# The head of the first load by two queues, and the second load as one transfer

## The chip, the cores and the metric

The kernel runs on one core of a Trainium2 chip. The time is device microseconds of that core, as the median of several executions: 83.15 us over 7 runs, from 82.97 to 83.2. One more execution was profiled. It took 83.2 us itself, and the profile covers 81.4 us of it, from the first instruction to the last; all times inside the kernel are counted from the start of that span.

## The reference

The input is a matrix of 1024 rows and 4096 columns in float32. Each row has its mean taken off and every element is squared:

```python
mean = np.mean(x, axis=axis, keepdims=True)
return ((x - mean) ** 2).astype(np.float32)
```

So 16.78 MB are read from HBM, 16.78 MB are written, and a row's result can't be started until the whole row is there.

## The kernel before

The rows are taken as two tiles of 512 rows. In a tile each of the 128 partitions holds four whole rows one after the other, 4 x 4096 floats or 64 KiB, which lie side by side in HBM too. Both tiles fit into SBUF at once, so each has its own buffer (`bufs=ntiles`), nothing is used twice, and results overwrite the inputs in place.

All loads are issued ahead of any work, from two engines' DMA queues. The queue of SP (SyncE) is called q1 in the profile and that of ACT (ScalarE) q10. In the order of each queue:

- SP, line 52: the head of tile 0, the first 512 floats (2 KiB) of each partition.
- SP, line 53: the rest of tile 0, 62 KiB of each partition.
- SP, line 57: all of tile 1 but its last 512 floats, 62 KiB of each partition.
- ACT, line 56: the tail of tile 1, the last 2 KiB of each partition. It is the first thing in ACT's program.

Then the loops run over the two tiles and over the four rows of a partition. DVE (VectorE) adds the two halves of a row and sums them with the factor -1/4096, so that one instruction gives the negative mean (line 66). ACT squares the row with that number as its bias (line 77). Of each tile's fourth row ACT squares only the first 3584 columns; DVE does the last 512 (lines 86 and 87). When a tile's four rows are done, SP stores it in one DMA of 64 KiB a partition (line 88).

The first instruction on a tile waits for every DMA of the tile that it needs. For tile 0 that is the head and the rest together, since row 0 is 16 KiB wide and the head is only 2 KiB of it. The tail of tile 1 is needed only by that tile's fourth row. The stores wait in SP's queue until the last squares of their tile are written; behind the second store is nothing but the end of the program. The order on each engine is that of the program text: DVE's is held by `keep_in_program_order`, and the others follow their dependences.

Of the kernel before, what the change touches and what calls it, by code (L numbers as in the profile page):

```python
# [2 lines left out]

os.environ.setdefault("NEURON_RT_ULTRASERVER_MODE", "4")

# [4 lines left out]

F32 = mybir.dt.float32
ACT = mybir.ActivationFunctionType
ADD = mybir.AluOpType.add


@with_exitstack
def kernel(
    ctx: ExitStack,
    tc: tile.TileContext,
    x: bass.AP,  # L20
    axis: bass.AP,
    out: bass.AP,
):

    nc = tc.nc

    B, D = x.shape
    P = nc.NUM_PARTITIONS
    Q = 4
    HEAD = 512
    HALF = D // 2
    LAST = D - D // 8
    assert B % (P * Q) == 0
    ntiles = B // (P * Q)
    inv_d = 1.0 / float(D)

    x_t = x.rearrange("(p n q) d -> n p (q d)", p=P, q=Q)
    out_t = out.rearrange("(p n q) d -> n p (q d)", p=P, q=Q)

    io = ctx.enter_context(tc.tile_pool(name="io", bufs=ntiles))
    scratch = ctx.enter_context(tc.tile_pool(name="scratch", bufs=1))
    stats = ctx.enter_context(tc.tile_pool(name="stats", bufs=ntiles * Q))

    tiles = []
    for i in range(ntiles):
        x_tile = io.tile([P, Q * D], F32)  # L50
        if i == 0:
            nc.sync.dma_start(out=x_tile[:, :HEAD], in_=x_t[i][:, :HEAD])  # L52
            nc.sync.dma_start(out=x_tile[:, HEAD:], in_=x_t[i][:, HEAD:])  # L53
        else:
            end = Q * D - HEAD
            nc.scalar.dma_start(out=x_tile[:, end:], in_=x_t[i][:, end:])
            nc.sync.dma_start(out=x_tile[:, :end], in_=x_t[i][:, :end])
        tiles.append(x_tile)

    inorder = tc.keep_in_program_order  # L60
    for i in range(ntiles):
        for q in range(Q):
            row = tiles[i][:, q * D:(q + 1) * D]
            pairs = scratch.tile([P, HALF], F32)
            neg_mean = stats.tile([P, 1], F32)
            inorder(nc.vector.tensor_tensor_reduce(  # L66
                out=pairs,
                in0=row[:, :HALF],
                in1=row[:, HALF:],
                scale=-inv_d,  # L70
                scalar=0.0,
                op0=ADD,
                op1=ADD,
                accum_out=neg_mean,
            ))
            cut = D if q < Q - 1 else LAST
            nc.scalar.activation(  # L77
                out=row[:, :cut],
                in_=row[:, :cut],
                func=ACT.Square,  # L80
                bias=neg_mean,
                scale=1.0,
            )
            if cut < D:
                rest = row[:, cut:]
                nc.vector.tensor_scalar_add(out=rest, in0=rest, scalar1=neg_mean)  # L86
                nc.vector.tensor_mul(out=rest, in0=rest, in1=rest)  # L87
        nc.sync.dma_start(out=out_t[i], in_=tiles[i])


# [1 line left out]
_INS = ['x', 'axis']  # L92
_OUTS = [((1024, 4096), 'float32')]

_NUMBERS = {'axis': -1}


# [26 lines left out]
```

## Time and profile before

| What | Value | Where it is read |
|---|---|---|
| median of 7 runs | 83.15 us (82.97 to 83.2) | the times |
| profiled execution | 83.2 us | the times |
| its span | 81.4 us | head of the page |
| DVE busy | 20.8 us (25%) | part 1 of the page |
| ACT busy | 29.4 us (36%) | part 1 |
| DMA moved | 33.55 MB, 412 GB/s over the span | part 3 |
| first DMA issued | 0.73 us | timeline |
| store of tile 0 issued | 39.71 us | timeline |
| store of tile 1 issued | 58.3 us | answer for line 88 |

The row of digits after "DMA" cuts the span into 40 slices of about 2 us. A packet is counted in the slice in which it starts, and most packets here last longer than 2 us, so a low digit between two nines isn't idle time: the packets of all 16 DMA engines begin close together, and some slices hold fewer beginnings. The mean over ten or more slices can be trusted, a single slice can't. The same holds for the GB/s row and for short windows.

### The profile page before, as it was taken

The page shows a single profiled execution, that of the slowest core. Times are in us where ns is not written, and L with a number is a line of the kernel's source. Part 1 is how long each engine was busy: PE and PEld are TensorE (multiplying, and loading weights), DVE is VectorE, ACT ScalarE, POOL GpSimd, SP SyncE. Part 2 cuts the span into 40 slices and gives each one's busy share as a digit, 9 for nine tenths or more (in the row PEclk, how much of TensorE's full clock was granted, in tenths as well). Part 3 has the DMA queues.
Part 4 walks back from the last instruction along what each step waited for, and adds up shares of the span by engine and source line. Part 5 has one row for each costly group of instructions (what it writes and reads, how often), then busy time and mean ns, then how long its engine had stood idle before and what let it go on. Part 6 is the DMA issues. An engine that isn't in the chain of part 4 may idle for free.

```text
span 81.4 us, 87 instructions
## 1 busy us (share of the span) xinstructions
DVE 20.8 (25%) x20; ACT 29.4 (36%) x9; POOL 0.2 (0%) x4
## 2 busy tenths in 40 slices
DVE  0000000000059999500049999700000000000000
ACT  0000000000054999999402999999600000000000
POOL 0000000000000000000000000000000000000000
DMA  1994999999839999996599997599999299999480
GB/s 24 701 437 187 405 499 499 499 499 468 374 156 499 499 499 499 499 468 281 250 515 515 515 515 322 225 483 515 515 515 483 97 451 515 515 515 483 193 354 0
DMA packets 864, 33.55 MB, mean 412 GB/s; under 512 B 96, under 2 KB 96, under 8 KB 352
## 3 DMA queue, kind: packets, MB, share of 16 engines
q1 hardware_dynamic: 720, 33.29, 94.8%
q10 hardware_dynamic: 144, 0.26, 1.0%
HBM read 16.78 MB, written 16.78 MB: 412 GB/s over the span
## 4 chain that ended last, share of the span: by engine, by line
DMA 49%; ACT 13%; ACTq 4%; DVE 3%; SPq 1%; issue 0%
DMA x_tile<-in_x_dram 49%; ACT x_tile L77 13%; ACTq L119 4%; DVE pairs L66 3%; SPq L53 1%; SPq L52 0%; DVE neg_mean L66 0%
## 5 line engine op out<-in xcount | busy, mean ns | idle before, releaser
L77 ACT ACTIVATE x_tile<-x_tile,neg_mean 128x4096 f32<-128x4096 f32 (+1 forms) x8 | 28.2, 3590 | 5.6 <-DVE neg_mean L66 5.6
L66 DVE CUSTOM_DVE_ANT_0 pairs<-x_tile 128x2048 f32<-128x2048 f32 x8 | 18.3, 2292 | 31.6 <-DMA x_tile<-in_x_dram 31.3
L77 ACT ACT_TABLE_LOAD x1 | 1.3, 1283 | 23.2 <-DMA x_tile<-in_x_dram 23.2
L87 DVE TENSOR_TENSOR x_tile<-x_tile 128x512 f32<-128x512 f32 x2 | 1.4, 693 | 0.1
L86 DVE TENSOR_SCALAR x_tile<-x_tile,neg_mean 128x512 f32<-128x512 f32 x2 | 1.0, 487 | 0.1
L66 DVE DVE_READ_ACCUMULATOR2_ANT neg_mean<- 128x1 f32 x8 | 0.7, 82 | 0.0
L105 POOL MEMSET const-bfloat16-1.0<- 128x1 bf16 x1 | 0.1, 101 | 0.0
L105 POOL MEMSET const-uint8-127<- 128x1 uint8 x1 | 0.1, 101 | 0.0
L105 POOL MEMSET const-float32-0.0<- 128x1 f32 x1 | 0.1, 98 | 0.2 <-issue 0.2
L105 POOL MEMSET const-float32-1.0<- 128x1 f32 x1 | 0.1, 98 | 0.0
## 6 DMA issues: line engine op xcount, KB each, us to landing
x_tile<-in_x_dram SPq DMA_DIRECT2D x2, 7936.0 KB, 31.1
x_tile<-in_x_dram SPq DMA_DIRECT2D x1, 256.0 KB, 3.6
x_tile<-in_x_dram ACTq DMA_DIRECT2D x1, 256.0 KB, 3.8
out_dram<-x_tile SPq DMA_DIRECT2D x2, 21.9
```

What stands on the lines that cost most here:

```text
L53: nc.sync.dma_start(out=x_tile[:, HEAD:], in_=x_t[i][:, HEAD:])
L66: inorder(nc.vector.tensor_tensor_reduce(out=pairs, in0=row[:, :HALF], in1=row[:, HALF:], scale=-inv_d, scalar=0.0, op0=ADD, op1=ADD, accu ...
L77: nc.scalar.activation(out=row[:, :cut], in_=row[:, :cut], func=ACT.Square, bias=neg_mean, scale=1.0,)
L86: nc.vector.tensor_scalar_add(out=rest, in0=rest, scalar1=neg_mean)
L87: nc.vector.tensor_mul(out=rest, in0=rest, in1=rest)
L105: nc = _bacc.Bacc("TRN2", target_bir_lowering=False, num_devices=1)
L119: with _tile.TileContext(nc) as tc:
```

## The change

The head of tile 0 is still the first 2 KiB of each partition. It now comes as two DMAs: SP issues it for partitions 0 to 63, ACT for partitions 64 to 127. ACT no longer issues a tail for tile 1. Tile 1 is one DMA on SP, 64 KiB a partition. The rest of tile 0 stays as it was, second in SP's queue. There are four loads before and after, three from SP and one from ACT. One empty line of the source falls away as well, and the loop of the head is a line longer, so that later line numbers are lower by one in the changed kernel.

```diff
         if i == 0:
-            nc.sync.dma_start(out=x_tile[:, :HEAD], in_=x_t[i][:, :HEAD])
+            for queue, p in ((nc.sync, 0), (nc.scalar, P // 2)):
+                part = slice(p, p + P // 2)
+                queue.dma_start(out=x_tile[part, :HEAD], in_=x_t[i][part, :HEAD])
             nc.sync.dma_start(out=x_tile[:, HEAD:], in_=x_t[i][:, HEAD:])
         else:
-            end = Q * D - HEAD
-            nc.scalar.dma_start(out=x_tile[:, end:], in_=x_t[i][:, end:])
-            nc.sync.dma_start(out=x_tile[:, :end], in_=x_t[i][:, :end])
+            nc.sync.dma_start(out=x_tile, in_=x_t[i])
         tiles.append(x_tile)
```

The first instruction on tile 0 now waits for three DMAs (two halves of the head and the rest) where it waited for two. The first on tile 1 waits for one, which brings the fourth row's tail too. The order of the instructions on DVE, ACT and POOL is unchanged; only the sizes of the DMAs that SP and ACT issue differ.

## The prediction

> **What bounds the kernel now.** I read the page first, then the chain that ended last, the timeline of the issues, the waits of SP's queue, and last the single DMA packets of the trace. The page, part 1 to 3:
>
> ```profile
> DVE 20.8 (25%) x20; ACT 29.4 (36%) x9; POOL 0.2 (0%) x4
> ...
> DMA  1994999999839999996599997599999299999480
> ...
> q1 hardware_dynamic: 720, 33.29, 94.8%
> q10 hardware_dynamic: 144, 0.26, 1.0%
> ```
>
> No engine works half of the time, and the packets of the two queues fill 95.8% of all 16 DMA engines' span. What little they leave lies at the two ends. The chain that ended last (start, length, what):
>
> ```profile
> 1.15 0.43 SPq L53
> 1.58 0.05 issue
> 1.63 40.25 DMA x_tile<-in_x_dram
> ...
> 41.90 2.29 DVE pairs L66
> ```
>
> It runs through the second load (landing at 41.88) and then over DVE and ACT. That tail is misleading, because the second store has slack, as SP's waits (total, times, longest) and the timeline (start, length) show:
>
> ```profile
> SPq L119 <- DMA out_dram<-x_tile: 21.8, 2, 19.3
> SPq L88 <- ACT x_tile L77: 11.7, 2, 5.8
> ```
>
> ```profile
> 0.73 0.38 SPq L52 DMA_DIRECT2D x_tile<-in_x_dram  x1
> 0.73 0.40 ACTq L56 DMA_DIRECT2D x_tile<-in_x_dram  x1
> 1.15 0.43 SPq L53 DMA_DIRECT2D x_tile<-in_x_dram  x1
> 1.63 0.42 SPq L57 DMA_DIRECT2D x_tile<-in_x_dram  x1
> ```
>
> At the end SP waits for a store 21.8 us, 19.3 of them in one piece: transfers end the kernel, not arithmetic. The last store is issued at 58.31, while the packets of the first store drain from the 16 engines only between 60.15 and 60.94.
>
> The packet records settle it. Each DMA engine runs 16 packets of 2 KiB (eight of the head, eight of the tail), then eight of 62 KiB, eight more of 62 KiB, and twice eight of 64 KiB. Once an engine has begun its first long packet, the next begins as the one before ends: 2.342 us for 62 KiB, 2.418 us for 64 KiB, with at most 0.4 us of idle time on the few engines that wait for the first store. The last completion record of an engine lies between 79.47 and 80.28; the span ends 1.14 us after the latest. So the end is the start of the slowest engine plus a fixed amount of work. The 16 engines begin their first long packet between 3.34 and 4.07, and the one at 4.07 (the next is at 3.87) is also the one that ends at 80.28. How they come to that point, by windows (the last two columns: share of the DMA engines, GB/s):
>
> ```profile
> 1.10:1.70 0.60, 0.00 (x0) 0.00 (x0) 0.00 (x0) 1.00 0.00 0
> 1.70:2.30 0.60, 0.00 (x0) 0.00 (x0) 0.00 (x0) 1.00 0.71 147
> 2.30:3.30 1.00, 0.00 (x0) 0.00 (x0) 0.00 (x0) 1.00 0.99 338
> ```
>
> First packet 1.74 (1.01 us after the issue at 0.73), for ACT's queue 1.97; a slow 0.6 us, with single packets of 0.3 to 0.56 us; from 2.3 full. Within the full stretch a 2 KiB packet follows the last after 0.080 us. Only what happens before about 4 us, and the bytes, can move the time.
>
> **What the Trainium skill says.** "DMA: Bandwidth & Descriptors", section "Issuing engines are not separate DMA queues": transfers from SP and ACT run on the same 16 engines and interleave. The trace agrees: on the engine that starts last, packets of q1 and q10 alternate every 0.080 us. The same page, "Why a DMA increments its semaphore by 16 and not by 1": a transfer uses the largest number of engines up to 16 that divides its slowest dimension, so 64 partitions should still use 16, with four packets each; no run shows that yet. Its "Rules for kernel authors" say of two transfers to disjoint partition halves: "Don't bother — they serialize". And "SBUF — State Buffer", section "Door 1", gives 196 GB/s for partitions 0 to 63 alone (8 ports) against 328 GB/s for 128, both at 1 MiB. The kernel before has no half-width transfer, so its trace can't confirm these two.
>
> **The change, part by part**, on one DMA engine.
>
> 1. The tail leaves ACT's queue. Eight packets of 2 KiB go: 8 x 0.080 = 0.64 us less.
> 2. Tile 1 comes as packets of 64 KiB: 8 x (2.418 - 2.342) = 0.61 us more. The 2.418 is measured on stores; 2.342 x 64/62 = 2.418 says the same for loads.
> 3. The head stays at eight packets (four from each queue, 8 x 0.080 = 0.64). A second completion record comes with each half, as the tail had one: nothing.
> 4. SP's and ACT's issues: each queue keeps its number of DMAs, at 0.38 to 0.43 us each, so the rest of tile 0 is issued at about 1.15 and tile 1 at 1.63, as now. Nothing is moved past another instruction. If a 64-partition issue is shorter, SP's later ones gain some 0.1 us at most. ACT's table load behind its DMA waits until 23.2 for tile 0, which hides anything there.
> 5. Waits: the first DVE instruction needs three DMAs instead of two. The head halves land near 4 us, the rest at about 22.6, so the added wait is long met. Behind it is DVE's whole work, but the rest decides. Row 3 of tile 1 gets its tail with the load at 41.9 instead of early; DVE reaches that row only at 48.90, so this is covered by 7 us, and row 0 waits for that same load now as before.
> 6. What comes earlier: tile 0 lands 0.64 us sooner (23.2 to about 22.6), as no tail packets stand before it, and its store is issued at about 39.07 instead of 39.71. The first packet of this store came 1.13 us after its issue, on other engines up to some 1.55. Now the load of tile 1 is drained at 40.83 to 41.50 and a few engines wait up to 0.4 us; afterwards the store is ready in time everywhere. The slowest engine did not wait (its gap was 0.02), so this is worth nothing to the end. Tile 1's chain, landing to store in 58.31 - 41.88 = 16.43 us, keeps its length and its slack.
> 7. The unknown: is the engine fed when only 0.64 us of small packets stand before the rest of tile 0? Before, it had 1.28. The rest was issued at 1.15; with the delay of the head (1.01) and of the slowest engine of the store (1.55) its descriptors are there at 2.16 to 2.70. The earliest small packets start at 1.74, the slowest engines' near 2.07, and slow first packets add about 0.4 us on average (first long packet at 3.57 on average, less 1.85 for the start and 1.29 for the packets). So small packets last until 2.4 at the least, about 2.9 in the mean. I take the bubble as nothing. Ends: if descriptors came only at the moment at which each long packet now starts, the whole 0.61 us would be lost. On the other side, [...]the slowest engine could fall back in line with the next one: 4.07 - 3.87 = 0.2 us gained.
>
> Sum: -0.64 + 0.61 = -0.03 us. From the profiled 83.2 that is 83.17; this execution lies 0.05 above the median, so against the 83.15 shown it is 83.12.
>
> **The rivals.**
>
> *Slower: the start isn't filled.* The place is 1.7 to 4.1 us on the slowest engine, the price up to +0.61 us (83.76), and it counts from the point at which that engine's first long packet starts later than 4.07 - 0.61 = 3.46. The mechanism is the half-width transfer: if two halves share what eight ports take, 262 KB at 196 GB/s last 1.34 us (estimate from "SBUF — State Buffer") instead of 0.64. Since long packets for all partitions join at 2.2 to 2.7, only about 0.6 us of that is at half speed: +0.3 us, 83.45. For it: the page's rule, and ACT's queue starting 0.23 us late, so that SP's half is alone at first. Against it: the two queues together cover all partitions, and the first 0.6 us run at 147 GB/s anyway, below the 196 of one half.
>
> *Faster: a more even start.* Half as many descriptors for each queue and half as many slow small packets bring the slowest engine to its first long packet 0.2 us nearer to the others: -0.03 - 0.2 gives 82.92. For it: the end follows one straggler, 0.25 us behind the next engine (80.28 against 80.04). Against it: long single packets come with the first accesses of each engine on each queue, and both queues stay.
>
> *The tail's removal exposes a wait.* Tile 1 lands later as its load is longer by 0.61 us, so the second store starts later. The landing, 41.88, is the sum over an engine of the same bytes, so it doesn't move; the slack of 60.15 - (58.31 + 1.55) = 0.3 us on the first engine covers it. Time 83.12, not to be told from the main case.
>
> **How the numbers follow.** Main case (with the last rival) 53 in 100, its own range 82.99 to 83.31, which is within 0.2% or 0.17 us of the median, about what a measurement of this kernel can tell from no change. Slower 30, 83.32 to 83.76 and mostly near 83.45. Faster 17, 82.85 to 82.98. The range that leaves out about 2 in 10 cuts the outer part of both: 82.92 to 83.55.
>
> **What would show it.** Right: q1 with 656 packets and q10 with 80 (16 engines for each half); tile 0 landing near 22.6 and its store issued near 39.1; tile 1 landing at 41.8 to 42.0; long packets back to back from about 3.4 on the slowest engine; the last store issued near 58.3. Wrong: fewer completions for a half (then it uses fewer engines); gaps between small and first long packets, or small packets of 0.16 us (the ports); a first long packet after 3.6 on the slowest engine; a store of tile 1 that finds its engines idle near 60. A changed time with the start at 3.4 and the landing at 41.9 would refute the whole reading, for it would come from the stores.

## The result, and the profile after

The changed kernel takes 83.51 us (median of 13 runs, 83.28 to 84.47) against 83.14 for the kernel before (33 runs, 82.92 to 83.37). The ratio is 1.0065, with a 95% interval from 1.0047 to 1.0084: slower by about half a microsecond in the mean and by 0.37 in the median. The ratios here and below compare means and leave out single executions more than 1.5% above the fastest of their kernel, which the medians keep. The stated range held the time, but only in the part that a rival with another mechanism had put there; the likeliest case, no measurable change, was wrong.

The profiled execution took 83.44 us with a span of 81.6, so it shows 0.24 us of the loss. The page of the changed kernel, parts 1 to 3:

```profile
DVE 20.8 (25%) x20; ACT 29.4 (36%) x9; POOL 0.2 (0%) x4
...
DMA  0997499999938999974999992999995599999190
...
q1 hardware_dynamic: 656, 33.42, 95.2%
q10 hardware_dynamic: 80, 0.13, 0.5%
```

The arithmetic is the same to the digit. The packets are the 656 and 80 that 16 engines for each half give. The DMA row now begins with a 0 in its first slice where the kernel before had a 1. The timeline of the issues (start, length, queue and line) says a part of why:

```profile
0.72 0.54 SPq L53 DMA_DIRECT2D x_tile<-in_x_dram  x1
0.72 0.55 ACTq L53 DMA_DIRECT2D x_tile<-in_x_dram  x1
1.31 0.56 SPq L54 DMA_DIRECT2D x_tile<-in_x_dram  x1
1.94 0.42 SPq L56 DMA_DIRECT2D x_tile<-in_x_dram  x1
```

The kernel before issued its head in 0.38 us, the tail in 0.40 and the rest of tile 0 in 0.43. A half of the head, with half the bytes, keeps its queue for 0.54 or 0.55 us, and the DMA behind it on SP, which is the same as before, takes 0.56. Only tile 1's is back at 0.42. By windows (last two columns: share of the DMA engines, GB/s) nothing moves before 2 us:

```profile
1.70:2.00 0.30, 0.00 (x0) 0.00 (x0) 0.00 (x0) 1.00 0.00 0
2.00:2.30 0.30, 0.00 (x0) 0.00 (x0) 0.00 (x0) 1.00 0.88 177
```

SP's first packet starts at 2.04 instead of 1.74, ACT's at 2.40 instead of 1.97. On SP 0.16 us of the 0.30 are the longer issue; the rest lies between the end of the issue and the first packet, and what it is the trace doesn't show. The chain and the waits of SP's queue after:

```profile
1.94 40.29 DMA x_tile<-in_x_dram
42.23 0.02 issue
42.25 2.29 DVE pairs L65
```

```profile
SPq L118 <- DMA out_dram<-x_tile: 21.7, 2, 19.3
SPq L87 <- ACT x_tile L76: 11.7, 2, 5.8
```

Tile 1 lands at 42.23 instead of 41.88, and the end still waits 19.3 us in one piece for a store. The packet records, as the mean over the 16 engines and for the last of them, make the balance:

```
us                                before   after
first packet of the kernel          1.74    2.04
tile 1 loaded, mean of engines     41.05   41.56
tile 1 loaded, last engine         41.50   41.87
last store done, mean of engines   79.84   80.20
last store done, last engine       80.28   80.51
```

On the average engine 0.30 us come from the later first packet and 0.20 more arise during the loads: the first long packet takes 0.31 us longer than before and the last one of tile 1 0.07 longer than the other seven (2.49 against 2.418), while the small packets pass 0.13 quicker than their number alone would give. Behind the loads 0.15 come back: 0.08 since tile 0's store is there when the loads end (its first packet follows the last load at once, before 0.09 us later), the rest in slightly shorter store packets (2.418 instead of 2.422). That makes +0.35, and +0.23 on the engine that ends last in these two executions.

The engine that ends last isn't in both the one with the latest start. Before, the engine that begins its first long packet last, at 4.07, is also the one that ends last. After, the one that begins last, at 3.65, ends at 80.32. The one that ends last, at 80.51, began at 3.17, but its first long packet took 2.85 us where 2.342 is the rule, and its last of tile 1 2.58 instead of 2.418.

### The profile page after: what moved, and what is told of

The parts are those of the page before. It is cut to its first block, busy times and chain, and to the rows that moved or that the text cites. A ratio compares the mean times of both kernels' runs of the same rounds, so it can differ in the third digit from the quotient of the medians.

```text
span 81.6 us, 87 instructions
## 1 busy us (share of the span) xinstructions
DVE 20.8 (25%) x20; ACT 29.4 (36%) x9; POOL 0.2 (0%) x4
## 4 chain that ended last, share of the span: by engine, by line
DMA 49%; ACT 13%; ACTq 4%; DVE 3%; SPq 1%; issue 0%
DMA x_tile<-in_x_dram 49%; ACT x_tile L76 13%; ACTq L118 4%; DVE pairs L65 3%; SPq L54 1%; SPq L53 1%; DVE neg_mean L65 0%
```

## The experiments

Two theories stood at first. *Issue*: DMAs of 64 partitions are slow to issue and so start late. *Cover*: with 0.26 MB of small packets ahead of the long ones instead of 0.52 MB, the first long packets are slow; they took 2.67 us on average in the changed kernel against 2.36 in the kernel before. The ratios, each with the runs of before on the same chip:

| Run | Median us | Ratio | 95% interval |
|---|---|---|---|
| after_again | 83.55 | 1.0075 | 1.0047 to 1.0102 |
| split_tail | 83.89 | 1.0101 | 1.0081 to 1.0121 |
| whole_one | 83.48 | 1.0033 | 1.0018 to 1.0049 |
| cols_one | 83.14 | 1.0014 | 1.0003 to 1.0025 |
| one_later | 83.48 | 1.0068 | 1.0036 to 1.0099 |
| halves_sp | 85.72 | 1.0338 | 1.0319 to 1.0356 |
| tail_halves | 83.88 | 1.0104 | 1.0086 to 1.0121 |
| w96_32 | 83.21 | 1.0024 | 1.0009 to 1.0038 |
| whole_4k | 83.36 | 1.0037 | 1.0024 to 1.0050 |
| halves_4k | 83.89 | 1.0097 | 1.0084 to 1.0110 |
| plain | 83.21 | 1.0017 | 1.0009 to 1.0025 |
| whole_again | 83.42 | 1.0039 | 1.0021 to 1.0057 |
| cols_4k | 83.22 | 1.0026 | 1.0015 to 1.0038 |
| w80_48 | 83.24 | 1.0030 | 1.0016 to 1.0044 |
| quarters | 84.14 | 1.0121 | 1.0096 to 1.0145 |
| cols_4k_late | 83.23 | 1.0007 | 0.9995 to 1.0020 |
| cols_4k_again | 83.21 | 1.0008 | 0.9996 to 1.0021 |

**The changed kernel once more.** There is no edit.

> The changed kernel once more, for a second profile and its spread. Both theories expect it 0.3 to 0.6 us (0.4 to 0.7%) above the kernel before, SP's first issue at 0.54 us where the whole head took 0.38, and the first packet at 2.04 us against 1.74. If the 0.54 was a chance of one execution, the issue falls back to about 0.4 here.

SP's first issue is 0.54 us again, ACT's 0.55, the rest of tile 0 0.56; the first packet starts at 2.05. The ratio agrees with the first one. The slow issue is not a chance of one execution.

**Half of the change: the head whole, or cut by columns.** Diffs against the changed kernel:

```diff
 whole_one
-            for queue, p in ((nc.sync, 0), (nc.scalar, P // 2)):
-                part = slice(p, p + P // 2)
-                queue.dma_start(out=x_tile[part, :HEAD], in_=x_t[i][part, :HEAD])
+            nc.sync.dma_start(out=x_tile[:, :HEAD], in_=x_t[i][:, :HEAD])
 cols_one
-            for queue, p in ((nc.sync, 0), (nc.scalar, P // 2)):
-                part = slice(p, p + P // 2)
-                queue.dma_start(out=x_tile[part, :HEAD], in_=x_t[i][part, :HEAD])
+            for queue, c in ((nc.sync, 0), (nc.scalar, HEAD // 2)):
+                cols = slice(c, c + HEAD // 2)
+                queue.dma_start(out=x_tile[:, cols], in_=x_t[i][:, cols])
```

> The head whole on SP as before, tile 1 as one DMA, nothing on ACT's queue: the other half of the change alone. Theory 'half-width DMAs start late': first packet at 1.74 again, time within 0.15 us of before. Theory 'too little small work ahead': only 0.26 MB stands before the long packets, so first long packets take 2.6 us on average again and the time is 0.3 to 0.5 us above before.

> The head over the same two queues with the same bytes, but halved by columns (all 128 partitions, 1 KiB each from SP and from ACT), tile 1 as one DMA. Theory 'half-width DMAs start late': issues of 0.38 to 0.40 us, first packet at 1.74, time within 0.2 us of before. Theory 'too little small work ahead': 0.3 to 0.5 us above before, with slow first long packets. If two queues at once are the cost, whatever the shape, it equals the changed kernel.

Both issue in 0.38 to 0.39 us and start at 1.74. Their first long packets are slow nevertheless (2.68 and 2.70 us on average). Yet cols_one is only 0.14% above before: two queues at once, and first long packets as slow as these, don't make the changed kernel's loss. whole_one lies between the two theories; its 20 runs fall into a group from 83.02 to 83.17 and one from 83.44 to 83.75, with one at 85.35.

**The other half: the split head with before's tail.** Against the changed kernel, tile 1 as in the kernel before, its tail by ACT behind ACT's half of the head.

```diff
-            nc.sync.dma_start(out=x_tile, in_=x_t[i])
+            end = Q * D - HEAD
+            nc.scalar.dma_start(out=x_tile[:, end:], in_=x_t[i][:, end:])
+            nc.sync.dma_start(out=x_tile[:, :end], in_=x_t[i][:, :end])
```

> The head split over two queues by partitions as in the changed kernel, but tile 1 with its own 2 KiB tail on ACT's queue as before (behind ACT's half of the head). Theory 'half-width DMAs start late': the issues take 0.54 us again, the first packet comes at 2.04, and the time is 0.3 to 0.5 us above the kernel before. Theory 'too little small work ahead of the long packets': the cover is back at 0.5 MB, first long packets take 2.34 us again, and the time is within 0.15 us of before.

The ratio is 1.0101, and its interval overlaps that of the changed kernel: the tail at its old size brings nothing back. The timeline of its issues:

```profile
0.72 0.56 ACTq L53 DMA_DIRECT2D x_tile<-in_x_dram  x1
0.72 0.56 SPq L53 DMA_DIRECT2D x_tile<-in_x_dram  x1
1.32 0.86 ACTq L57 DMA_DIRECT2D x_tile<-in_x_dram  x1
1.33 0.57 SPq L54 DMA_DIRECT2D x_tile<-in_x_dram  x1
```

The full-width tail behind a half takes 0.86 us to issue, where 0.40 was enough at the head of the queue. So the cover was not restored at all: the tail's packets come after the first long ones and lie between them until 23 us. There they cost 0.077 us each on average, no more than ahead of the long ones, which stay at 2.342. The slow issues speak for the issue theory; about cover the run tells nothing.

**Is it the width?** w96_32 and w80_48 cut the head at another partition, quarters in four; halves_sp puts both 64-wide halves on SP with the rest as in the kernel before; tail_halves leaves SP's queue as before and cuts ACT's tail in halves.

```diff
 w96_32 (w80_48: 80 in place of 96), against the changed kernel
-            for queue, p in ((nc.sync, 0), (nc.scalar, P // 2)):
-                part = slice(p, p + P // 2)
+            for queue, part in ((nc.sync, slice(0, 96)), (nc.scalar, slice(96, P))):
 quarters, against the changed kernel
+            for queue, part in ((nc.sync, slice(0, 32)), (nc.scalar, slice(32, 64)),
+                                (nc.sync, slice(64, 96)), (nc.scalar, slice(96, P))):
 halves_sp, against the kernel before
-            nc.sync.dma_start(out=x_tile[:, :HEAD], in_=x_t[i][:, :HEAD])
+            for p in (0, P // 2):
+                part = slice(p, p + P // 2)
+                nc.sync.dma_start(out=x_tile[part, :HEAD], in_=x_t[i][part, :HEAD])
 tail_halves, against the kernel before
-            nc.scalar.dma_start(out=x_tile[:, end:], in_=x_t[i][:, end:])
+            for p in (0, P // 2):
+                part = slice(p, p + P // 2)
+                nc.scalar.dma_start(out=x_tile[part, end:], in_=x_t[i][part, end:])
```

> The changed kernel with the head cut at partition 96 instead of 64: 96 partitions by SP, 32 by ACT. If any width other than 128 is slow to issue, both first issues take about 0.54 us, the first packet comes at 2.04 and the time equals the changed kernel's (83.5). If the count of partitions matters, SP's issue lies between 0.38 and 0.54 and ACT's is above 0.55.

> The changed kernel with the head cut at partition 80: 80 partitions by SP, 48 by ACT. If 64 alone is slow to issue, both issues take about 0.39 to 0.41 us, the first packet comes at 1.74, and the time is near 83.2. If only widths that 32 divides are fast, they take 0.54 us and the time is 83.5.

The timeline of w96_32:

```profile
0.73 0.39 SPq L52 DMA_DIRECT2D x_tile<-in_x_dram  x1
0.73 0.41 ACTq L52 DMA_DIRECT2D x_tile<-in_x_dram  x1
1.17 0.42 SPq L53 DMA_DIRECT2D x_tile<-in_x_dram  x1
```

Its first packet starts at 1.74, and w80_48 reads the same (0.39, 0.41, 0.42, first packet 1.74). Nothing but the place of the cut differs from the changed kernel, and the ratio falls from 1.0065 to 1.0024 and 1.0030: some 0.3 us, the lateness of the first packet. In w96_32 the average engine's last store is done at 79.83, as before (79.84), against 80.20 in the changed kernel. Of the widths tried (32, 48, 80, 96, 128) none is slow to issue; 64 is, at partition 0 and at partition 64, on SP and on ACT. Why 64 is slow no run shows.

> The head as two half-width DMAs both on SP, one after the other; tile 1's tail on ACT and the rest as before. Theory 'a half-width DMA is slow to issue, and so is the one behind it': SP's first three issues take about 0.54, 0.54 and 0.56 us, the first packet of q1 comes at 2.04, ACT's issue stays at 0.40 with its packets at 1.97; time 0.2 to 0.6 us above before. Rival 'it is the two queues issuing half-width DMAs together': SP's issues are 0.38 and 0.43 us, the first packet at 1.74, time within 0.2 us.

> The kernel before, with ACT's tail of tile 1 as two half-width DMAs; SP's queue is untouched. Theory 'issue': ACT's two issues take 0.54 us and more, its packets come at 2.3 or later, SP's first packet stays at 1.74, and the time is within 0.2 us of before, since SP's head covers the start. Rival 'half-width transfers share eight ports and hold up the engines': 2 KiB packets of 0.16 us and a time 0.3 us above before.

In halves_sp SP alone issues halves:

```profile
0.72 1.18 SPq L53 DMA_DIRECT2D x_tile<-in_x_dram  x2
0.73 0.36 ACTq L57 DMA_DIRECT2D x_tile<-in_x_dram  x1
1.95 0.58 SPq L54 DMA_DIRECT2D x_tile<-in_x_dram  x1
2.57 0.44 SPq L58 DMA_DIRECT2D x_tile<-in_x_dram  x1
```

Two halves take 1.18 us and the DMA behind them 0.58, while ACT's full-width tail stays at 0.36: the rival of two queues issuing halves together falls. Here the size expected was far off: 85.72 us, 2.7 above before. SP's first packet comes at 2.42 where 2.04 was expected, which stays unexplained, the first long packets between 3.32 and 5.67, tile 0 is complete only at 25.37, its store is issued at 42.34, and the engines stand idle 0.9 us on average between load and store.

tail_halves contradicts the issue theory as I had put it, that halves off the first queue are free. SP starts at 1.72, but the time is 0.8 us above before. Its DMA issues (queue, count, size of each, median us to landing):

```profile
x_tile<-in_x_dram ACTq DMA_DIRECT2D x2, 128.0 KB, 10.5
x_tile<-in_x_dram SPq DMA_DIRECT2D x1, 256.0 KB, 3.0
```

The second half of the tail comes so late that its packets lie between long packets of SP's queue until 16 us, and each engine's second to fifth long packets take about 2.44 us instead of 2.342, some 0.4 us in all. That small packets lie among long ones isn't enough for it, since in split_tail the long ones stayed at 2.342; what makes the difference no run shows. In both runs the median 2 KiB packet took 0.084 us; the 0.16 us that the rival of the ports expects don't show.

> The head as four DMAs of 32 partitions, two on SP and two on ACT. If the width 64 is the cost, all issues take about 0.38 to 0.43 us, the first packet comes at 1.74, and the rest of tile 0 is issued one DMA later, at about 1.6. The time is then at or below the changed kernel's (83.2 to 83.5). If any DMA narrower than 96 is slow on SP, SP's two take 0.54 us each and the time is above 84.

quarters issues quickly (two in 0.84 us on SP, two in 0.88 on ACT, the rest of tile 0 at 1.62) and starts at 1.73, but takes 84.14. I had expected no more than the changed kernel's time. The issue of width 32 is not the cost. The rest of tile 0 is issued 0.45 us later than in w96_32, and the first long packets are slower (2.6 to 3.75 us, 3.06 on average against 2.59); the average engine ends 0.46 us later, at 80.29. So a late rest of tile 0 is the likely cost here, which no run tests alone.

**What makes the first long packets slow, and does it matter?**

```diff
 one_later, against whole_one
         else:
+            nc.vector.tensor_copy(out=x_tile[:, :1], in_=tiles[0][:, :1])
             nc.sync.dma_start(out=x_tile, in_=x_t[i])
 whole_4k against whole_one, halves_4k against the changed kernel, cols_4k against cols_one
-    HEAD = 512
+    HEAD = 1024
 plain, against the changed kernel: no head, each tile one DMA on SP
-        ... (the whole `if i == 0:` and `else:`)
+        nc.sync.dma_start(out=x_tile, in_=x_t[i])
```

> Head whole on SP, tile 1 as one DMA, but issued only once the head has landed (a copy of one column by DVE, overwritten later, makes it wait), so near 4 us instead of 1.63. If the slow first long packets (2.4 to 2.9 us in place of 2.34) come from the issue of tile 1's descriptors at the same time, they are 2.34 us here and the time is 83.0 to 83.1, at or below the kernel before. If they come from the ramp after the first access, they stay at 2.6 to 2.8 us and the time is that of the whole head with one tile-1 DMA (83.1 to 83.6).

The issue of tile 1 moves to 3.57 us, and the first long packets still take 2.63 on average: it is not tile 1's issue that slows them. The delay itself brings nothing: the ratio is above whole_one's, and the two intervals overlap.

> Head whole on SP, tile 1 as one DMA, but a head of 4 KiB a partition in place of 2 KiB, so that 0.52 MB stand before the long packets as in the kernel before. If the rest of the loss is too little cover at the start, the first long packets take 2.34 us, as before, and the time is within 0.15 us of the kernel before. If the tail's place on a second queue is what counts, it stays 0.2 to 0.4 us above before with slow first long packets.

> The changed kernel with a head of 4 KiB a partition: two 64-partition halves of 0.26 MB each. If slow issue (0.54 us) and too little cover add up, the issues and the first packet (2.04) stay, the first long packets are 2.34 us, and the time is 0.3 us above before, some 0.2 us below the changed kernel. If the issue time came from the size of 2 KiB rows, it is 0.38 us here.

> No head and no tail: each tile one DMA of 64 KiB a partition on SP. The cover theory expects the slowest start of all full-width forms: first long packets at 1.74 that take 2.8 us or more, and a time 0.3 us or more above before. If a head is of no use, the time is within 0.15 us of before, since the bytes are the same.

With 4 KiB ahead the first long packets (60 KiB now) of whole_4k are nearly clean on all engines but one, but the time stays at 1.0037. halves_4k keeps its 0.54 us issues and gets slower, not faster (1.0097). Its first long packets stay slow (2.61 us on average, where 2.267 is the rule) in spite of the cover, and its 4 KiB packets take 0.23 us in the mean against 0.20 in whole_4k. That is the one place where halves show slower packets; as SP's took 0.163 us in the median from 2.3 to 2.6 us, while no packet of ACT had started, against 0.162 in whole_4k in the same stretch, a doubling by the ports doesn't explain it. Without any head the first long packets start at 1.74 and take 3.02 us, and the kernel is only 0.17% above before. So the cover theory falls: more bytes ahead don't always make the first long packets quick, and where they do, the time does not follow. whole_4k's profiled execution, the slowest of its runs at 84.17, shows what made that one slow. The engine that ends last, followed back packet by packet (start, length in us; 60 KiB at 2.267 and 64 KiB at 2.418 are the rule):

```
first long packet    3.71   3.20
last one of tile 1  39.66   2.98
last store done     81.27        (mean of the engines: 79.97)
```

All its other long packets are within 0.01 us of the rule.

> The whole head with one tile-1 DMA once more: its times fell into two groups, near 83.1 and near 83.55, and the profile was of the first. A profile of the second group should show where 0.45 us comes in: at the start (the first long packets of one engine later than 3.5 us), or later (long packets slower than 2.42 us, or gaps, in one of the stores).

The two groups of whole_one became a scatter from 83.06 to 84.8. The profile is of the slowest execution, far from both groups, so it can't say what separates them. This stays open.

**The best start, and the early store.**

```diff
 cols_4k_late, against cols_4k: a needless copy in place ahead of tile 0's store
+        if i == 0:
+            nc.scalar.activation(out=tiles[i][:, :HEAD // 2], in_=tiles[i][:, :HEAD // 2],
+                                 func=ACT.Copy)
         nc.sync.dma_start(out=out_t[i], in_=tiles[i])
```

> Head of 4 KiB a partition, halved by columns: 2 KiB from SP and 2 KiB from ACT for all 128 partitions, tile 1 as one DMA. The start is then packet for packet that of the kernel before (0.52 MB of 2 KiB packets over two queues), but all of it belongs to tile 0, so its store is issued near 39.1. If the start over two full-width queues is what the kernel before has over the others, the average engine ends 0.15 us earlier than before and the time is 82.9 to 83.05, at or below before. If one long load for tile 1 costs in itself, it is 0.15 to 0.4 us above before.

> Head of 4 KiB by columns over two queues, tile 1 as one DMA, and one needless copy of 512 columns in place by ACT (about 0.6 us) ahead of tile 0's store, so that the store is issued near 39.7 as in the kernel before instead of 39.1. If the early store disturbs the last long packets of the load, the excess falls away and the time is 82.95 to 83.1 with the narrow spread of before. If the rest comes from the start, nothing changes against cols_4k (83.2, up to 83.75).

> The same without the copy, once more on the same chip, as the partner of the late store: 83.2 with a spread up to 83.7. A profile of one of its slower executions should show either one engine far behind the others from its first packets on (start), or slow long packets at 38 to 41 us on many engines (store).

cols_4k starts as the kernel before does, and its profiled execution (83.03) ends 0.18 us earlier on the slowest engine (80.10 against 80.28). Yet its 22 runs reach 83.75 and the ratio is 1.0026 on one chip, and 1.0008 on the next. The late store changes nothing in the time (1.0007, with the store at 39.76; in the profiled execution of its partner tile 0 came late and the store went out at 39.67 by itself). The traces show something all the same. With the store issued at 39.01 (cols_4k) the last packet of tile 1 takes 2.56 us on the average engine, with the copy ahead of the store 2.418. In the other forms with tile 1 as one DMA it takes 2.51 to 2.70 where the store is issued by 39.1, and at most 2.46 from 39.67 on. So an early store closes the gap behind the load and goes with a longer end of the load, and in sum no gain is measured. In the profiled execution of cols_4k_again (83.61) one engine's first long packet takes 3.02 us where the others take 2.27, and, followed in the same way, it is the one that ends last, with no other slow packet. What remains of the loss without the slow issue, 0.1 to 0.4% by form, chip and execution, goes in the two profiles that show it with single engines that stall at the start, and in whole_4k once more at the end of the load. That leaves out one_later and quarters, which issue something late. I haven't found what triggers the stalls, nor a form that beats the kernel before: of the changed kernel's 0.65% the issue of the halves explains a little more than half, and the rest stays open.

## Why the prediction was wrong

*What bounds the kernel*: right in the main. The late first packet reached the end, and a store was the last wait. But "the start of the slowest engine plus a fixed amount of work" doesn't hold: the first long packet and the last of the load vary, and the engine with the latest start was not the one that ended last.

*Steps 1 to 3, packets*: right as far as they go. The packet counts came out as given, and a loaded 64 KiB packet takes 2.418 us as estimated. The mean start of the first long packet (3.59 before; the prediction has 3.57) moved to 3.12.

*Step 4, the issues*: this failed. It took 0.38 to 0.43 us for each DMA from rows of 128 partitions and allowed only for a shorter issue at 64. No row of before had a 64-partition DMA, so the cost had to be bounded from both sides, and I bounded it on the good side only. It measured 0.54 and 0.55 us, 0.56 for the DMA behind it, and the first packet came 1.31 us after the start of its issue instead of 1.01, 0.30 us later in the kernel. The cut at 96 or 80 takes that back and more than half of the loss with it.

*Step 5, waits*: right; DVE begins on tile 0 at 22.90, when the rest has landed, before 23.27.

*Step 6, the early store*: about right in its worth, not in how. The store was issued at 39.34, between the 39.07 expected and the 39.71 of before, and the idle time ahead of it vanished. On the average engine 0.15 us came back behind the loads, and the last packet of the load took 0.07 longer.

*Step 7, the bubble*: wrong too, and smaller. The last small packet of any engine, with the completion record behind it, ends at 3.21, so the engine that begins its first long packet at 3.65 stood idle for at least 0.44 us, and the one at 3.37 for at least 0.16. Neither is the engine that ends last. On the others the long packets follow at once, or nearly, but the first takes 2.67 us on average. The loads on the average engine lost 0.20 us beyond the late start, and the experiments don't tie that to the cover.

*The rivals*: the slower one had the place, the start, and nearly the time, 83.45, by luck. Its point of decision was 3.46 on the slowest engine; 3.65 was measured, which would make +0.19, near the +0.23 at the end, but on another engine than the one that ended last. Its mechanism, ports shared by half the partitions, was wrong: the median 2 KiB packet takes 0.084 us in both kernels. The warning of the Trainium skill about two partition halves ("DMA: Bandwidth & Descriptors", "Rules for kernel authors") held as advice. Its reason is that both halves run on the same 16 engines; the completions agree (16 for each half), but that says only that nothing is gained. The loss that the runs show comes from the issue of that width. The faster rival, a more even start, did not come. The third, an exposed wait for the second store, did not either: that store's first packets follow the first store's last without a gap.

## What to carry to other kernels

Where the DMA engines are busy from the first packet to the last, a late first packet is paid at the end; read the issue time of each early DMA in the timeline. A new shape of DMA needs a price of its own, slower as well as faster, even when it carries fewer bytes. And when a bound is read from the slowest engine, follow that engine packet by packet after the change too: it may be another one, late for another reason.

## What was not expected of the hardware

- A DMA of 64 partitions took 0.53 to 0.62 us to issue on SP and on ACT, and the full-width DMA behind it 0.56 to 0.86, where loads of 32, 48, 80, 96 and 128 partitions not behind one took 0.33 to 0.45.
- The first long packet on an engine took mostly 2.4 to 3.3 us where the later ones take 2.27 to 2.42, but not in the kernel before (2.36 on average) or in the forms with 4 KiB ahead at full width (2.27 to 2.35). The time doesn't follow it simply: cols_one has 2.70 on average and is 0.14% above before, quarters has 3.06 and is 1.2% above.
- The last packet of the load took 2.56 us instead of 2.418 on the average engine when the first store had been issued at 39.01 (cols_4k) instead of 39.76 (cols_4k_late).
- In two profiled executions a single engine with a first long packet of 3.0 or 3.2 us set the end of all 80 us behind it.
